# Gate and up products of a feed-forward block: a weight sum by an accumulating transfer, six wide products in 17 blocks, and two pairs of products with their wide matmuls in one row

## The chip, the cores and the metric

The kernel runs as one program on one NeuronCore of a Trainium2 chip. Its engines are TensorE (PE, its weight loads PEld), VectorE (DVE), ScalarE (ACT), GpSimd (POOL) and SyncE (SP); each takes its own instructions in order, and semaphores join them. The metric is the device time of one execution in microseconds, the median of several runs.

## The reference

One decoder layer on a 512 x 1024 stream in float32. The change lies in its third sublayer, the SwiGLU feed-forward with a hidden width of 2816:

```python
hf = rms_norm(x, norm_ffn[l])
gate, up = jnp.split(hf @ w_ffn_in[l], 2, axis=-1)
x = x + (jax.nn.silu(gate) * up) @ w_ffn_out[l]
return rms_norm(x, norm_final)
```

The parts before it (a mixer of stick-breaking attention and a short convolution, then a cross-attention into 256 memory tokens) are the same in both kernels.

## The kernel before

Every float32 product is made from a high and a low part in a rounded 32-bit format: high x high, high x low, low x high. ScalarE casts the high part, VectorE subtracts it from the source to get the low part (`rest_of`, line 1005). The gate and up weights are worked in 22 blocks of 128 hidden columns (`NF`), one block m after another. A block's product is a 2 x 2 matrix of submatrices over two halves of the contraction and of the tokens, and it is computed with seven half-size products (Winograd's form of Strassen's method), numbered 0 to 6. The token side of the seven (`x2f`, made by `forms_of`, line 699) is ready before the stage.

Weight side of block m. `ffn_load` (line 847) loads `wg` (two submatrices) and `ws` (one submatrix twice) on SP's queue and accumulates two more into `ws` with a transfer on POOL's queue. `load_corner` (line 865) loads the submatrix a22. Three VectorE or transfer sums make the rest: `sum_third` (line 872) overwrites the first half of `wg` with the weight of product 3, and `sum_last` (line 876) adds the two halves of `wg` into the second half of the corner tile. Casts: `pair_cast(m, 0)` makes the weights of products 0 and 1 from `wg`, `pair_cast(m, 1)` those of 4 and 2 from `ws`, `pair_cast(m, 2)` those of 5 and 6 from the corner tile, `third_cast` that of 3. There are six input buffers for `wg` and `ws`, three blocks' worth.

A product (line 902) has four steps k over the contraction. A narrow product issues three matmuls of 256 columns in each: 12. Where the token side stands as high and low part beside each other, it is wide: one matmul of 512 columns with the weight's high part, and later one of 256 with its low part: 4 and 4. A wide product leaves two halves in the bank that must be added when it is read. Products 1, 2 and 6 are wide in all blocks, 5 in the blocks of `WIDE` (5 to 18), the others narrow.

Banks: products 0, 3, 4 and 5 accumulate in one PSUM bank z, product 1 has v, products 2 and 6 accumulate in y. After each of 0, 3, 4 ScalarE copies what z holds (`reads`, line 939; with 5 wide, its upper half too), since the running sums are needed; VectorE adds those copies to y and v (`joined_halves`, line 935, two 256-wide additions). `evict` (line 956) scales the gate by the norm's factor (part 0), takes silu on ScalarE (part 1) and multiplies with up (part 2).

The order is written by hand: `uses` (line 980) is the order of products, for a block m

```python
[(m, 3), (m, 2), (m, 4), (m + 1, 0), (m + 1, 1), (m, 5), (m, 6)]
```

and `todo` holds, by place in `uses`, what ScalarE and VectorE do behind that product; `made(n, cast, ...)` puts a cast at place n and its low part one place later. TensorE, ScalarE and VectorE keep this order exactly. In what follows "a block" of the order is one such row of seven products.

Of the kernel before, what the change touches and what calls it, by code (L numbers as in the profile page):

```python
# [44 lines left out]
def hybrid_layer(ctx: ExitStack, tc: tile.TileContext, xT_d, memT_d, mem_d, cols_d, wv_d, win_d,  # L45
# [653 lines left out]
    def forms_of(xe, xo):  # L699

        b11, b12, b21, b22 = xe[:, :HS], xe[:, HS:], xo[:, :HS], xo[:, HS:]
        c, d = f(unit("c1")), f(unit("c2"))
        n1, t3, n2, t4 = c[:, :HS], c[:, HS:], d[:, :HS], d[:, HS:]
        nc.vector.tensor_tensor(out=n1, in0=b11, in1=b12, op=ALU.subtract)
        nc.vector.tensor_tensor(out=t3, in0=b22, in1=b12, op=ALU.subtract)
        nc.vector.scalar_tensor_tensor(out=n2, in0=n1, scalar=-1.0, in1=b22, op0=ALU.mult,  # L708
                                       op1=ALU.subtract)
        nc.vector.scalar_tensor_tensor(out=t4, in0=n2, scalar=-1.0, in1=b21, op0=ALU.mult,  # L710
                                       op1=ALU.subtract)
        u = unit("xf")
# [12 lines left out]
        third, fifth = beside(n2, "xd"), beside(t4, "xd")  # L725
        last = beside(b22, "xo")
        return [(u[:, a], u[:, b]), first, second, third[:2], fourth[:2], fifth, last]

    def residual(w_dram, act, old, gain, pairs=False):

# [112 lines left out]

    KP = KD // 2
    raws, corners = {}, {}

    def ffn_load(m):

# [26 lines left out]

    def sum_last(m, eng=nc.vector):
        wg = raws[m][0]
        eng.tensor_tensor(out=corners[m][:, 1, :], in0=wg[:, 0, :], in1=wg[:, 1, :], op=ALU.add)

    wforms = {}  # L880

    def pair_cast(m, which):

        raw = (*raws[m], corners[m])[which]
        hi = wpool.tile([P, 2, 512], F32R, tag="wh", name=nm("wf"))
        lo = wpool.tile([P, 2, 512], F32R, tag="wl", name=nm("wf"))
        nc.scalar.copy(hi, raw)
# [14 lines left out]
    def product(ps, m, i, ks=range(KP)):  # L902

        rests = []
        for k in ks:
            hi, lo = (w[:, k * P:(k + 1) * P] for w in wforms[m, i])
            xh, xl, *both = x2f[k][i]
            if both and (i != 5 or m in WIDE):
                nc.tensor.matmul(ps, hi, both[0], start=i < 3 and k == 0, stop=False,  # L909
                                 skip_group_check=True)  # L910
                rests.append((ps[:, :HS], lo, xh))
                continue
            for j, (a, b) in enumerate(((hi, xh), (hi, xl), (lo, xh))):
                nc.tensor.matmul(ps[:, :HS], a, b, start=i < 3 and k == 0 and j == 0,  # L914
                                 stop=k == KP - 1 and j == 2, skip_group_check=True)
        for operands in rests:
            nc.tensor.matmul(*operands, start=False,  # L917
                             stop=ks[-1] == KP - 1 and operands is rests[-1],
                             skip_group_check=True)

    WIDE = range(5, NF - 3)
    banks, silus = {}, []
    acts = {}

# [14 lines left out]
    def reads(m, i):  # L939

        b = banks[m]
        z, s, t = b["z"][:, :HS], b["s"], b["t"]
        if i == 5 and m in WIDE:
            nc.scalar.copy(s[:, :HS], b["z"][:, HS:])
        elif i in (0, 3, 4):
            nc.scalar.copy((s[:, :HS], None, None, s[:, HS:], t[:, :HS])[i], z)  # L946
        elif i == 1:
            joined_halves(b["g"][:, :HS], b["v"], s[:, :HS])
        elif i == 6:
            joined_halves(b["g"][:, HS:], b["y"], s[:, HS:])  # L950

    def second(m):
        b = banks[m]
        joined_halves(b["t"][:, HS:], b["y"], b["t"][:, :HS])

    def evict(m, part):
# [6 lines left out]
        else:  # L963
# [3 lines left out]
            to = slice(odd * HS, (odd + 1) * HS)  # L967
            first = b["z"][:, :HS]
            if m in WIDE:
                first = b["s"][:, :HS]  # L970
# [8 lines left out]

    uses = [(0, 0), (0, 1), (0, 2), (1, 0), (1, 1), (0, 3), (1, 3), (0, 4), (1, 2), (0, 5), (0, 6),  # L980
            (1, 4), (2, 0), (2, 1), (1, 5), (1, 6)]
    for m in range(2, NF - 1):
# [158 lines left out]
    for m in range(1, NF - 1):  # L1141
        p = {i: uses.index((m, i)) for i in range(2, 7)}
        q = {i: uses.index((m + 1, i)) for i in range(2)}
        if m > 1:
            at(p[3], lambda m=m: sum_third(m + 1))
            at(p[3], lambda m=m: evict(m - 1, 0))
            at(p[2], lambda m=m: evict(m - 1, 1))
            at(q[0], lambda m=m: evict(m - 1, 2))
            made(p[3], pair_cast, m, 2)
            made(p[2], third_cast, m + 1)  # L1150
        else:
            made(p[4], third_cast, m + 1)
        at(p[4], lambda m=m: second(m))
        if m + 2 < NF:
            at(p[4], lambda m=m: load_corner(m + 2))
        made(q[0], pair_cast, m + 1, 1, late=2)
        at(q[1] if m < NF - 2 else p[4], lambda m=m: sum_last(m + 1))
# [36 lines left out]
    with tc.manual_schedule(engines={mybir.EngineType.PE, mybir.EngineType.Activation,  # L1194
# [6 lines left out]
        for n, (m, i) in enumerate(uses):  # L1201
            if n == 3:
                product(banks[m]["z"], m, i, range(KP - 1, KP))
            elif n > 3:
                product(bank_of(m, i), m, i)
            reads(m, i)
            for part in todo.get(n, ()):
                part()
            if n == 6:
                mean2 = mean2()  # L1210
            elif n == 8:
                mean2 = mean2[0]("r0b", bank=mmtile, later=True)
            elif n == 9:
                r2b[0] = mean2()
                turn_r2()
# [319 lines left out]
```

## Time and profile before

| | |
|---|---|
| median of 3 runs | 839.92 us (839.05 to 839.99) |
| profiled execution | 838.75 us, its span 837.0 us |
| mean granted TensorE clock | 0.998 |
| gate and up stage | from 502 to 721 us of the span, 22 blocks |
| busy in the span: PE, DVE, ACT, POOL | 828.8, 684.6, 463.9, 161.2 us |

A row of the timeline gives start and length of equal instructions that follow each other, then engine, line, operation, out<-in and shape, and in brackets the engine's idle time before it and what ended it. Names are without buffer numbers: z, y, v are banks, sa, sb and fg VectorE's and ScalarE's working tiles, wf a weight form, wg, ws and a the weight tiles (a: the corner tile), xf, xo, xc, xd the token forms. A group row gives the count, the busy time and, after the comma, the mean length of one in ns. The length of a matmul is longer than its distance to the next, since matmuls overlap; starts are compared instead. A block is the time from one product 3 to the next.

### The profile page before, as it was taken

What the parts mean: (1) busy time and instruction counts of PE and PEld (TensorE: products, weight loads), DVE (VectorE), ACT (ScalarE), POOL (GpSimd) and SP (SyncE); (2) the same over time, 40 slices, a digit from 0 to 9 for tenths busy, and PEclk for the clock granted to TensorE, in tenths of its full rate; (3) what the DMA queues carried; (4) which work ended last, traced back from release to release, by engine and by line L of the source; (5) the groups of instructions that cost most, each with busy time, mean ns of one, the idle gap of its engine ahead of it and who ended that gap; (6) DMA issues with size and microseconds to landing.
All of it is one profiled execution on the core that took longest, in us unless ns stands there. A gap on an engine that the chain in (4) does not pass through costs nothing.

```text
span 837.0 us, 11962 instructions
## 1 busy us (share of the span) xinstructions
PE 828.8 (99%) x4374; PEld 714.1 (85%) x4374; DVE 684.6 (82%) x1086; ACT 463.9 (55%) x796; POOL 161.2 (19%) x168
## 2 busy tenths in 40 slices
PE   9999999999999999999999999999999999999996
PEld 7888888888888888888888789999999999888885
DVE  7879899996756576587555698999999999999886
ACT  7567868674332355434444566645555555576654
POOL 0011131110566630173000031111111110000401
PEclk9999999999999999999999999999999999999999
DMA  8552435235687865566431326677767673465552
GB/s 303 155 166 101 122 111 103 74 115 174 228 312 276 304 249 188 182 233 249 148 82 51 101 51 161 167 184 200 197 180 197 176 184 95 170 213 197 180 183 101
DMA packets 51357, 143.69 MB, mean 172 GB/s; under 512 B 5761, under 2 KB 7041, under 8 KB 48482
## 3 DMA queue, kind: packets, MB, share of 16 engines
q1 hardware_dynamic: 41650, 107.89, 38.2%
q0 software_dynamic: 9360, 34.75, 15.8%
q8 instruction: 34, 0.56, 0.3%
q10 hardware_dynamic: 288, 0.28, 0.1%
q14 instruction: 25, 0.20, 0.1%
HBM read 125.20 MB, written 13.64 MB: 166 GB/s over the span
## 4 chain that ended last, share of the span: by engine, by line
PE 99%; DVE 0%; ACT 0%; DVEq 0%; issue 0%
PE z L914 13%; PE p L1228 12%; PE pr L161 8%; PE pr L162 8%; PE pr L163 8%; PE y L909 5%; PE r L162 3%; PE r L163 3%; PE r L161 3%; PE v L288 3%; PE y L917 2%; PE v L909 2%; PE km L666 2%; PE mq L163 2%; PE mq L161 2%; PE mq L162 2%
## 5 line engine op out<-in xcount | busy, mean ns | idle before, releaser
L156 ACT CAST wh<-wr 128x1024 fp32r<-128x1024 f32 x84 | 88.0, 1051 | 144.2 <-issue 80.0
L157 DVE TENSOR_TENSOR wl<-wr,wh 128x1024 fp32r<-128x1024 f32 x84 | 111.0, 1321 | 32.0 <-ACT wh L156 31.9
L161 PE MATMUL pr<-xgh,wh 128*128 128x512 f32 x288 | 112.8, 392 | 0.0
L162 PE MATMUL pr<-xgl,wh 128*128 128x512 f32 x288 | 112.4, 390 | 0.0
L163 PE MATMUL pr<-xgh,wl 128*128 128x512 f32 x288 | 112.3, 390 | 0.0
L611 POOL TENSOR_TENSOR pre<-pre 128x512 f32<-128x512 f32 x44 | 70.9, 1616 | 31.5 <-DMA pre<-in_w_ffn_out_dram 29.2
L862 POOL DMA_DIRECT2D ws<-in_w_ffn_in_dram x22 | 26.6, 1209 | 248.5 <-DVE c L708 54.0
L163 PEld LDWEIGHTS pr<-xgh,wl 128*128 128x128 f32 x288 | 54.1, 188 | 11.5
L161 PEld LDWEIGHTS pr<-xgh,wh 128*128 128x128 f32 x288 | 54.1, 188 | 10.6
L162 PEld LDWEIGHTS pr<-xgl,wh 128*128 128x128 f32 x288 | 54.1, 188 | 10.5
L914 PE MATMUL z<-xd,wf 128*128 128x256 f32 x360 | 47.5, 282 | 0.0
L946 ACT COPY sa<-z 128x256 f32<-128x256 f32 x44 | 16.4, 373 | 51.9 <-PE z L914 51.9
L914 PEld LDWEIGHTS z<-xd,wf 128*128 128x128 f32 x360 | 45.0, 190 | 0.1
L1006 DVE TENSOR_TENSOR wf<-wg,wf 128x1024 fp32r<-128x1024 f32 (+1 forms) x44 | 43.1, 978 | 1.5
L1006 DVE TENSOR_TENSOR wl<-wr,wh 128x1024 fp32r<-128x1024 f32 x33 | 41.0, 1242 | 1.8 <-ACT wh L1073 1.8
L1073 ACT CAST wh<-wr 128x1024 fp32r<-128x1024 f32 x33 | 34.5, 1050 | 5.3 <-ACT f01h L1002 2.6
L914 PE MATMUL z<-xf,wf 128*128 128x256 f32 x264 | 35.4, 283 | 0.0
L914 PE MATMUL z<-xc,wf 128*128 128x256 f32 x264 | 35.1, 283 | 0.0
L914 PEld LDWEIGHTS z<-xf,wf 128*128 128x128 f32 x264 | 33.4, 192 | 0.1
L914 PEld LDWEIGHTS z<-xc,wf 128*128 128x128 f32 x264 | 33.0, 190 | 0.0
L368 DVE TENSOR_TENSOR g<-pr,r0b 128x512 f32<-128x512 f32 x16 | 11.0, 687 | 23.5 <-PE pr L163 23.5
L417 POOL TENSOR_SCALAR_AFFINE_SELECT e<-e 128x128 f32<-128x128 f32 (+1 forms) x24 | 10.7, 447 | 86.6 <-DVE e L470 86.6
(356 smaller groups left out, 2239.9 us busy)
## 6 DMA issues: line engine op xcount, KB each, us to landing
wr<-in_w_in_dram SPq DMA_DIRECT2D x36, 512.0 KB, 3.4
pre<-in_w_ffn_out_dram POOLq DMA_DIRECT2D x11, 1024.0 KB, 8.0
sums<-pre POOLq DMA_DIRECT2D x11, 1024.0 KB, 5.0
ws<-in_w_ffn_in_dram SPq DMA_DIRECT2D x22, 512.0 KB, 4.8
wg<-in_w_ffn_in_dram SPq DMA_DIRECT2D x22, 512.0 KB, 4.7
ws<-in_w_ffn_in_dram POOLq DMA_DIRECT2D x22, 512.0 KB, 5.7
wr<-sums SPq DMA_DIRECT2D x22, 512.0 KB, 4.0
wr<-in_w_ffn_out_dram SPq DMA_DIRECT2D x16, 512.0 KB, 3.7
```

Source lines behind the costliest of these rows:

```text
L156: after(nc.scalar.copy(h2, raw), lead[-1:])
L157: lows.append(nc.vector.tensor_tensor(out=l2, in0=raw, in1=f(h2), op=ALU.subtract))
L161: nc.tensor.matmul(ps, a[0], b[0], start=start, stop=False, **kw)
L162: nc.tensor.matmul(ps, a[0], b[1], start=False, stop=False, **kw)
L163: nc.tensor.matmul(ps, a[1], b[0], start=False, stop=stop, **kw)
L611: nc.gpsimd.tensor_tensor(out=t[:, a, :], in0=t[:, a, :], in1=t[:, b, :], op=ALU.add)
L862: nc.gpsimd.dma_start(s13, a[:, 0:4:3, :], accum_op=ALU.add)
L909: nc.tensor.matmul(ps, hi, both[0], start=i < 3 and k == 0, stop=False, skip_group_check=True)
L914: nc.tensor.matmul(ps[:, :HS], a, b, start=i < 3 and k == 0 and j == 0, stop=k == KP - 1 and j == 2, skip_group_check=True)
L1006: nc.vector.tensor_tensor(out=lo, in0=src, in1=f(hi), op=ALU.subtract)
L1073: nc.scalar.copy(hi, raw)
L1228: nc.tensor.matmul(res[i][s2], a[:, ts], b, start=j == 0 and n == 0, stop=n == 2 and j == (BEHIND - 1 if (i, s2) == (5, 1) else NJ - 1))
```

## The change

Five things change, all in this stage.

1. In blocks 3 to 20 (`OWN`) `sum_last` is no VectorE addition but a transfer on POOL's queue, which accumulates the first half of `wg` onto its second half in place. `load_corner` then loads a22 over the first half of `wg` (SP's queue), so that `wg` itself becomes the source of `pair_cast(m, 2)`. The sum is issued behind `sum_third`, the corner load behind product 5 of the block before.
2. Products 3 and 4 are wide as well in the blocks of `WIDE`, which now are 3 to 19. There products 1 to 6 are wide, six of seven.
3. In these blocks ScalarE's copies behind 3 and 4 are 512 wide, and the two pairs of 256-wide additions on y become `folded`: one 512-wide addition of the bank and the copy, then one 256-wide addition of the two halves.
4. In these blocks the order is 3, 2, next block's 0, 4, next block's 1, 5, 6. Products 3 and 2, and 5 and 6, are issued together: eight 512-wide matmuls, then four 256-wide ones of the first and four of the second.
5. In `OWN` the cast of `pair_cast(m, 2)` moves from behind product 3 to behind product 4.

```diff
+    OWN = range(3, NF - 1)
...
     def load_corner(m):
+        if m in OWN:
+            nc.sync.dma_start(raws[m][0][:, 0, :], wfi_d[m][:, 3 * 512:])
+            return
...
     def sum_last(m, eng=nc.vector):
         wg = raws[m][0]
+        if m in OWN:
+            nc.gpsimd.dma_start(wg[:, 1, :], wg[:, 0, :], accum_op=ALU.add)
+            return
...
-        raw = (*raws[m], corners[m])[which]
+        raw = (*raws[m], raws[m][0] if m in OWN else corners[m])[which]
...
-            if both and (i != 5 or m in WIDE):
+            if both and (i not in (3, 4, 5) or m in WIDE):
...
-        for operands in rests:
-            nc.tensor.matmul(*operands, start=False,
-                             stop=ks[-1] == KP - 1 and operands is rests[-1],
-                             skip_group_check=True)
+        def ends():
+            for operands in rests:
+                nc.tensor.matmul(*operands, start=False,
+                                 stop=ks[-1] == KP - 1 and operands is rests[-1],
+                                 skip_group_check=True)
+        if later:
+            return ends
+        ends()
-    WIDE = range(5, NF - 3)
+    WIDE = range(3, NF - 2)
...
-        if i == 5 and m in WIDE:
-            nc.scalar.copy(s[:, :HS], b["z"][:, HS:])
+        if m in WIDE and i in (3, 4):
+            nc.scalar.copy((s, t)[i - 3], b["z"])
+        elif m in WIDE and i == 5:
+            nc.scalar.copy(t[:, :HS], b["z"][:, HS:])
+        elif m in WIDE and i == 6:
+            folded(b["g"][:, HS:], b["y"], s)
...
+    def folded(out_, bank, old):
+        nc.vector.tensor_tensor(out=old, in0=bank, in1=old, op=ALU.add)
+        nc.vector.tensor_tensor(out=out_, in0=old[:, :HS], in1=old[:, HS:], op=ALU.add)
...
     for m in range(2, NF - 1):
-        uses += [(m, 3), (m, 2), (m, 4), (m + 1, 0), (m + 1, 1), (m, 5), (m, 6)]
+        order = [(m, 3), (m, 2), (m, 4), (m + 1, 0), (m + 1, 1), (m, 5), (m, 6)]
+        if m in WIDE:
+            order[2:4] = order[3:1:-1]
+            beside_next |= {(m, 3), (m, 5)}
+        uses += order
...
             at(p[3], lambda m=m: sum_third(m + 1))
+            if m + 1 in OWN:
+                at(p[3], lambda m=m: sum_last(m + 1))
+                at(p[5], lambda m=m: load_corner(m + 1))
...
-            made(p[3], pair_cast, m, 2)
+            made(p[4] if m in OWN else p[3], pair_cast, m, 2)
...
+            elif uses[n - 1] in beside_next:
+                ends[1]()
+            elif (m, i) in beside_next:
+                ends = [product(bank_of(*use), *use, later=True) for use in uses[n:n + 2]]
+                ends[0]()
```

The instruction order of ScalarE over one block in the middle of the stage, before. z1211 is the bank of this block, z1229 that of the next; a221194 is this block's corner tile (its cast is that of `pair_cast(m, 2)`), wg1203 and ws1202 belong to the next block, wg1221 to the one after.

```order
L946 COPY sa1212_6153<-z1211_6152 128x256
L887 CAST wf1224_6234<-a221194_6037 128x1024
L962 ACTIVATE fg1201_6062<-fg1201_6062 128x512
L895 CAST wf1227_6248<-wg1203_6075 128x512
L946 COPY sb1213_6154<-z1211_6152 128x256
L946 COPY sa1230_6269<-z1229_6268 128x256
L887 CAST wf1232_6287<-ws1202_6073 128x1024
L944 COPY sa1212_6153<-z1211_6152 128x256
L887 CAST wf1238_6318<-wg1221_6191 128x1024
```

The same of the changed kernel. z1198 is the bank of this block, z1215 of the next; wg1178 is this block's `wg`, now the source of `pair_cast(m, 2)`; wg1193 and ws1192 belong to the next block, wg1210 to the one after.

```order
L957 COPY sa1199_6049<-z1198_6048 128x512
L986 ACTIVATE fg1191_5982<-fg1191_5982 128x512
L902 CAST wf1214_6153<-wg1193_5995 128x512
L963 COPY sa1216_6156<-z1215_6155 128x256
L894 CAST wf1218_6175<-ws1192_5993 128x1024
L957 COPY sb1200_6050<-z1198_6048 128x512
L894 CAST wf1220_6187<-wg1178_5891 128x1024
L959 COPY sb1200_6050<-z1198_6048 128x256
L894 CAST wf1226_6225<-wg1210_6102 128x1024
```

The cast of `pair_cast(m, 2)` stood second, behind the copy of product 3; now it stands behind the copy of product 4, and this copy behind that of the next block's product 0 and the cast of its `ws`.

VectorE from the low part of `pair_cast(m, 2)` to the additions of product 6, before (y1226 is the block's y, v1234 the next block's v, wf1225 the low part of the pair from a221194, wf1233 that from `ws` of the next block):

```order
L1006 TENSOR_TENSOR wf1225_6235<-a221194_6037,wf1224_6234 128x1024
L1006 TENSOR_TENSOR wf1227_6248<-wg1203_6075,wf1227_6248 128x512
L936 TENSOR_TENSOR sb1213_6154<-y1226_6237,sb1213_6154 128x256
L937 TENSOR_TENSOR sb1213_6154<-y1226_6237,sb1213_6154 128x256
L971 TENSOR_TENSOR sa1196_6040<-z1195_6039,sa1196_6040 128x256
L974 SCALAR_TENSOR_TENSOR a11214_6168<-sa1196_6040,fg1201_6062 128x256
L974 SCALAR_TENSOR_TENSOR a21215_6169<-sb1197_6041,fg1201_6062 128x256
L936 TENSOR_TENSOR fg1235_6291<-v1234_6290,sa1230_6269 128x256
L937 TENSOR_TENSOR fg1235_6291<-v1234_6290,fg1235_6291 128x256
L878 TENSOR_TENSOR a221210_6150<-wg1203_6075 128x512
L1006 TENSOR_TENSOR wf1233_6288<-ws1202_6073,wf1232_6287 128x1024
L936 TENSOR_TENSOR fg1219_6178<-y1226_6237,sa1212_6153 128x256
```

And of the changed kernel, from the additions of product 2 to the scaling that ScalarE's silu waits for (y1213 is the block's y, v1222 the next block's v, wf1221 the low part of the pair from wg1178, wf1219 that from `ws` of the next block, wf1227 that of the `wg` after):

```order
L970 TENSOR_TENSOR sb1200_6050<-y1213_6135,sb1200_6050 128x512
L971 TENSOR_TENSOR sb1200_6050<-sb1200_6050 128x256
L949 TENSOR_TENSOR fg1223_6193<-v1222_6192,sa1216_6156 128x256
L950 TENSOR_TENSOR fg1223_6193<-v1222_6192,fg1223_6193 128x256
L1035 TENSOR_TENSOR wf1221_6188<-wg1178_5891,wf1220_6187 128x1024
L1035 TENSOR_TENSOR wf1219_6176<-ws1192_5993,wf1218_6175 128x1024
L970 TENSOR_TENSOR sa1199_6049<-y1213_6135,sa1199_6049 128x512
L971 TENSOR_TENSOR fg1208_6089<-sa1199_6049 128x256
L1035 TENSOR_TENSOR wf1227_6226<-wg1210_6102,wf1226_6225 128x1024
L878 TENSOR_TENSOR wg1210_6102<-ws1209_6100,wg1210_6102 128x512
L984 TENSOR_TENSOR fg1208_6089<-fg1208_6089,r0b1034_4940 128x512
```

Before, the low part of this pair came first, ahead of the halves of product 2, the multiplications of the block before and the additions of v; now it comes behind the fold of product 2 and the additions of v. The addition L878 into the corner tile is gone, and the fold takes the place of the two halves.

More of the change, by code (lines that the diff above doesn't have):

```diff
@@ L726, in forms_of @@
         last = beside(b22, "xo")
-        return [(u[:, a], u[:, b]), first, second, third[:2], fourth[:2], fifth, last]
+        return [(u[:, a], u[:, b]), first, second, third, fourth, fifth, last]
     def residual(w_dram, act, old, gain, pairs=False):
@@ L900, in third_cast, with product @@
         return one_form(m, 3, *((fpool, "wg") if m == NF - 1 else (wpool, ("wh", "wl")[m % 2])))
-    def product(ps, m, i, ks=range(KP)):
+    def product(ps, m, i, ks=range(KP), later=False):
         rests = []
@@ L969, in evict @@
             if m in WIDE:
-                first = b["s"][:, :HS]
+                first = b["t"][:, :HS]
                 nc.vector.tensor_tensor(out=first, in0=b["z"][:, :HS], in1=first, op=ALU.add)
@@ L981, in hybrid_layer @@
             (1, 4), (2, 0), (2, 1), (1, 5), (1, 6)]
+    beside_next = set()
     for m in range(2, NF - 1):
-        uses += [(m, 3), (m, 2), (m, 4), (m + 1, 0), (m + 1, 1), (m, 5), (m, 6)]
+        order = [(m, 3), (m, 2), (m, 4), (m + 1, 0), (m + 1, 1), (m, 5), (m, 6)]
+        if m in WIDE:
+            order[2:4] = order[3:1:-1]
+            beside_next |= {(m, 3), (m, 5)}
+        uses += order
     m = NF - 1
@@ L1153, in hybrid_layer @@
         at(p[4], lambda m=m: second(m))
-        if m + 2 < NF:
+        if m + 2 < NF and m + 2 not in OWN:
             at(p[4], lambda m=m: load_corner(m + 2))
         made(q[0], pair_cast, m + 1, 1, late=2)
-        at(q[1] if m < NF - 2 else p[4], lambda m=m: sum_last(m + 1))
+        if m + 1 not in OWN:
+            at(q[1] if m < NF - 2 else p[4], lambda m=m: sum_last(m + 1))
         if m + 2 < NF:
```

2 lines of the change are left out of this document (added).

## Prediction

> **What bounds the kernel now.** I read the shares first, then the clock and the chain, then one block of the gate and up stage in order of time.
>
> ```profile
> PE 828.8 (99%) x4374; PEld 714.1 (85%) x4374; DVE 684.6 (82%) x1086; ACT 463.9 (55%) x796; POOL 161.2 (19%) x168
> PEclk9999999999999999999999999999999999999999
> PE 99%; DVE 0%; ACT 0%; DVEq 0%; issue 0%
> ```
>
> TensorE is never without work and the chain that ended last is TensorE alone. So the change gains only what it takes from TensorE, and loses whatever makes TensorE wait. The windows view gives the stage (502 to 721 us) and one block of it; its columns are length, PE, PEld, DVE, ACT, POOL, clock, DMA share, GB/s:
>
> ```profile
> 502.00:721.00 219.00, 219.00 (x1532) 204.79 (x1531) 210.53 (x365) 121.49 (x205) 25.33 (x23) 1.00 0.65 174
> 595.05:604.96 9.91, 9.91 (x70) 9.21 (x69) 9.55 (x18) 5.44 (x10) 1.20 (x1) 1.00 0.77 205
> ```
>
> VectorE works 9.55 of 9.91 us: there is no wait on PE, but almost no slack behind it. The same block in order of time, TensorE (start, length):
>
> ```profile
> 595.05 1.60 PE L914 MATMUL z<-xd,wf 128*128 128x256 f32 x12
> 596.48 1.09 PE L909 MATMUL y<-xc,wf 128*128 128x512 f32 x4
> 597.41 0.63 PE L917 MATMUL y<-xc,wf 128*128 128x256 f32 x4
> 597.88 1.59 PE L914 MATMUL z<-xc,wf 128*128 128x256 f32 x12
> 599.31 1.60 PE L914 MATMUL z<-xf,wf 128*128 128x256 f32 x12
> 600.75 1.09 PE L909 MATMUL v<-xo,wf 128*128 128x512 f32 x4
> 601.68 0.63 PE L917 MATMUL v<-xo,wf 128*128 128x256 f32 x4
> 602.15 1.09 PE L909 MATMUL z<-xd,wf 128*128 128x512 f32 x4
> 603.56 1.09 PE L909 MATMUL y<-xo,wf 128*128 128x512 f32 x4
> 604.96 1.59 PE L914 MATMUL z<-xd,wf 128*128 128x256 f32 x12
> ```
>
> From start to start a narrow product takes 1.43 us (595.05 to 596.48), a wide one 1.40 (596.48 to 597.88). Its four last, narrow matmuls take 0.47.
>
> **TensorE's gain.** 37 products turn wide: 3 and 4 in 17 blocks, 5 in three more (blocks 3, 4 and 19). At 0.03 us each that is 1.1 us. The new row order of wide matmuls saves nothing more: a wide matmul behind a narrow one starts at the same distance as behind a wide one (1.40 us for y, v and z alike). So 1.1 us is all that can be won, 0.13% of 839.92; about 0.2% is what a measurement of this kernel can tell from no change.
>
> **VectorE's balance.** Per block it loses one sum and gets two wide additions for four narrow ones:
>
> ```profile
> L1006 DVE TENSOR_TENSOR wf<-ws,wf 128x1024 fp32r<-128x1024 f32 x20 | 24.4, 1218 | 0.0
> L874 DVE TENSOR_TENSOR wg<-ws,wg 128x512 f32<-128x512 f32 x20 | 13.8, 692 | 0.6
> L960 DVE TENSOR_TENSOR fg<-fg,r0b 128x512 f32<-128x512 f32 x20 | 13.7, 685 | 0.0
> L878 DVE TENSOR_TENSOR a<-wg 128x512 f32<-128x512 f32 x20 | 13.6, 681 | 0.0
> L937 DVE TENSOR_TENSOR sb<-y,sb 128x256 f32<-128x256 f32 x21 | 8.9, 424 | 0.7
> L368 DVE TENSOR_TENSOR g<-pr,r0b 128x512 f32<-128x512 f32 x16 | 11.0, 687 | 23.5 <-PE pr L163 23.5
> 597.90 0.68 DVE L960 TENSOR_TENSOR fg<-fg,r0b 128x512 f32<-128x512 f32 x1
> 598.51 1.22 DVE L1006 TENSOR_TENSOR wf<-a,wf 128x1024 fp32r<-128x1024 f32 x1
> 600.41 0.42 DVE L936 TENSOR_TENSOR sb<-y,sb 128x256 f32<-128x256 f32 x1
> 600.86 0.42 DVE L937 TENSOR_TENSOR sb<-y,sb 128x256 f32<-128x256 f32 x1
> ```
>
> An instruction starts 0.08 us before the end of an independent one (598.51 against 597.90+0.68), and 0.03 after the end of one it depends on. A pair of halves costs 0.42+0.03+0.42; a fold (`folded`, one 512-wide addition, taken as 0.69 by L368, which also reads PSUM, then a 256-wide one) costs 0.69+0.03+0.42. Two folds add 0.54, the sum takes off 0.60. In total VectorE is as full as before; what matters is where its work stands.
>
> **Where the order goes wrong.** ScalarE in the same block:
>
> ```profile
> 596.68 0.37 ACT L946 COPY sa<-z 128x256 f32<-128x256 f32 x1 [1.46 <-PE z L914]
> 596.95 1.06 ACT L887 CAST wf<-a 128x1024 fp32r<-128x1024 f32 x1
> 598.62 0.64 ACT L962 ACTIVATE fg<-fg 128x512 f32<-128x512 f32 x1 [0.62 <-DVE fg L960]
> 599.16 0.60 ACT L895 CAST wf<-wg 128x512 fp32r<-128x512 f32 x1
> 599.67 0.37 ACT L946 COPY sb<-z 128x256 f32<-128x256 f32 x1
> 601.01 0.37 ACT L946 COPY sa<-z 128x256 f32<-128x256 f32 x1 [0.97 <-PE z L914]
> 601.27 1.05 ACT L887 CAST wf<-ws 128x1024 fp32r<-128x1024 f32 x1
> ```
>
> The second row is the cast for products 5 and 6. It ends at 598.01; product 5 starts at 602.15, 4.1 us later. The change puts this cast behind the copy of product 4, and the copy of product 4 behind product 0 of the next block. Between product 4 and product 5 TensorE now has one product, 1.40 us. In that time ScalarE must do: start 0.20 us after TensorE has gone on (596.48 to 596.68), copy 512 columns from PSUM, cast 1.06, and let TensorE restart. The nearest rows for the wide copy and the restart:
>
> ```profile
> L1273 ACT COPY s<-p 128x512 f32<-128x512 f32 x2 | 1.1, 584 | 0.0
> 460.16 0.59 ACT L179 CAST pth<-pt 128x512 fp32r<-128x512 f32 x1 [1.41 <-PE pt L829]
> 460.80 0.50 PE L161 MATMUL om<-pth,vmh 128*128 128x512 f32 x1
> L914 PEld LDWEIGHTS z<-xd,wf 128*128 128x128 f32 x360 | 45.0, 190 | 0.1
> ```
>
> The copy is 0.58, less 0.10 overlap with what follows it (599.16 against 598.62+0.64). The restart is 0.05 here, where the cast made the moving operand; a stationary one must also be loaded, up to 0.19 more. I take 0.13. Sum: 0.20+0.48+1.06+0.13 = 1.87 against 1.40: 0.47 us of idle TensorE in each of 17 blocks. Nothing covers it.
>
> **It closes a loop.** Behind that late cast VectorE makes the low parts, and behind those stands what feeds the next copy. One turn, following who waits for whom:
> - VectorE ends the scaling `evict(m-1, 0)`; ScalarE starts silu 0.04 later.
> - ScalarE: silu 0.64, third cast 0.60, copy of product 0 0.37, cast of `ws` 1.05, copy of product 4 0.58, less four overlaps of 0.10: 2.84.
> - VectorE: 0.04, fold of product 2 1.14, the two additions of product 1 0.87-0.08, low part of pair 2 1.22-0.08: 3.11.
> - TensorE, waiting for that low part: restart 0.13, the eight narrow matmuls of 5 and 6 0.94, read 0.20 later: 1.27 (VectorE's low part of the `ws` pair, 1.14, fits beside it).
> - VectorE: fold of product 6 1.14, low part of pair 0 1.22-0.08, `sum_third` 0.03+0.69, the scaling 0.69-0.08: 3.61.
>
> Sum 0.04+2.84+3.11+1.27+3.61 = 10.87 us for a block, where TensorE needs 6×1.40+1.43 = 9.83 and took 9.91. So 0.96 more in each of 17 blocks: 16.3 us, with the gain of the wide products already in it. Before, the cast stood two products earlier, so no such loop was closed.
>
> **The hand-over.** Block 20 keeps the old order of products but has the moved cast. From the end of its scaling to the low part that product 5 needs: silu and third cast 0.04+1.14; then on VectorE the third's low part 0.04+0.69, the halves of product 2 0.79, `sum_last(21)` 0.60, the three instructions of `evict(19, 2)` 0.33+0.45+0.34, the low part 1.14, restart 0.13: 5.7 us. The scaling ends 0.20+3.61 = 3.8 after the block begins, so the low part is there at 9.5; TensorE comes to it after 3 narrow and 2 wide products and two matmuls, 4.29+2.80+0.24 = 7.3. That is 2.2 us, once.
>
> **The sum transfer** itself I cost at nothing:
>
> ```profile
> L862 POOL DMA_DIRECT2D ws<-in_w_ffn_in_dram x17 | 20.5, 1208 | 141.4 <-DVE wf L1006 45.1 <-DVE sb L936 36.5 <-DMA ws<-in_w_ffn_in_dram 21.3
> ws<-in_w_ffn_in_dram POOLq DMA_DIRECT2D x17, 512.0 KB, 5.7
> a<-in_w_ffn_in_dram SPq DMA_DIRECT2D x19, 256.0 KB, 2.6
> ```
>
> It moves 256 KB with an addition: between 2.6 us (plain, same size) and 5.7 (accumulating, twice the size). I allow 5.7, then 2.6 for the corner's load that waits for it on SP's queue. It starts at the end of `sum_third`, 3.2 after a block begins; the cast that needs both starts 6.6 into the next block, 14.3 later. So 6 us are spare. Behind the corner's load on SP's queue stand the next `wg` and `ws` loads, which are first read a block later and more. On POOL's queue the accumulation into `ws` stands behind it, one issue (1.2) later; its `sum_third` comes a block later, 10.9, against 1.2+5.7 and the load in front of it. If that cover is gone, see the third rival. The same row shows POOL at 1.21 us per issue while VectorE is 96% busy. The Trainium skill (SBUF — State Buffer, "SBUF: two separate sides") speaks against such a transfer: GpSimd cannot write its descriptors while VectorE holds the shared port in a two-port operation. By that rule the sums would come late, and the time would be that of the third rival; the row shows no such hold.
>
> **Sum.** 838.75 (the profiled execution; its span is 837.0) + 16.3 + 2.2 = 857.25. That run lies 1.2 under the median of 839.92, so on the median: **858.4 us**. With a restart of 0.05 to 0.24 in the loop and the hand-over between 0 and 2.2 the bounds are 855 to 860.
>
> **Rivals.**
> 1. *Only the direct wait counts.* VectorE catches up, the loop doesn't close, each block loses 0.47: 8.0, less 1.1: 846.8. For it: VectorE's sum of work is no larger. Against it: its 9.55 of 9.91. Chance 0.08.
> 2. *No wait: the other side.* The cast comes in time and only the 1.1 stays: 838.8. This decides where copy and cast end within 1.40-0.13 = 1.27 us of product 4 and a turn takes under 9.83; my rows give 1.74 and 10.87. It would need ScalarE's in-order copy to be far shorter than L1273. Chance 0.04.
> 3. *The transfers are late.* If sum and corner take over 6 us more than allowed, or `ws` comes after its `sum_third`, VectorE waits too. `ws` issues on POOL already waited for loads (21.3 us in four or so blocks). Lateness of 1 to 6 us would be paid where the new scheme starts, less in later blocks, which are longer: 859.5 to 865. Chance 0.10.
> 4. *The clock falls.* With TensorE idle twice a block the granted clock could drop; at half speed 17 blocks of 9.83 take 167 us more, about 1025 us. The clock row holds 9 even in the last slice, where TensorE is busy 6 tenths. Chance 0.02. The Trainium skill (TensorE: Matmul & The Clock Gate, "A second HAM failure mode: psum-queue depth-cycling") describes frequent micro-idles that make the clock oscillate; no row here shows it.
>
> The forecast itself has 0.76. The range takes its bounds, most of the third rival, and on the low side a loop that closes only in part: 853 to 865. Under 838.2 nothing leads but an error in all of this: faster 0.01; same 0.03 (the second rival); slower 0.96.
>
> **What would show it.** Right: blocks of about 10.9 us in 17 of 22, two idle places of TensorE in each, the first before product 5 and ended by ScalarE's cast, the second, smaller, before its narrow matmuls and ended by VectorE; ScalarE's cast directly behind the copy of product 4. A wide product still 1.40. Wrong: blocks under 10 us, idle places ended by a DMA, or a clock under 9.

## The result, and the profile after

859.13 us, median of 4 runs (858.49 to 860.02), against 839.60 for the kernel before on the same chip: ratio 1.0234, 95% interval 1.0217 to 1.0250. The forecast was 858.4 (853 to 865). The profiled execution took 860.02, its span is 858.3, 21.3 more than before. From the page of the kernel after:

```profile
PE 838.8 (98%) x4226; PEld 707.6 (82%) x4226; DVE 686.3 (80%) x1071; ACT 470.6 (55%) x799; POOL 172.8 (20%) x186
PE 76%; DVE 15%; ACT 5%; issue 3%; DVEq 0%
```

The chain that ended last was TensorE alone before; now a quarter of it is other engines. VectorE's total has hardly moved (684.6 to 686.3): it isn't more work that costs, but where it stands. TensorE's waits in the whole span:

```profile
PE z L916 <- ACT wf L894: 8.5, 17, 0.5
PE z L921 <- DVE wf L1035: 1.9, 1, 1.9
```

Seventeen waits of 0.5 us for ScalarE's cast, one in each wide block, and one of 1.9 us in the hand-over. A block of the changed order on TensorE (start, length):

```profile
597.18 0.64 PE L926 MATMUL v<-xo,wf 128*128 128x256 f32 x4
598.32 1.20 PE L916 MATMUL z<-xd,wf 128*128 128x512 f32 x4 [0.50 <-ACT wf L894]
599.35 1.08 PE L916 MATMUL y<-xo,wf 128*128 128x512 f32 x4
600.48 0.74 PE L926 MATMUL z<-xd,wf 128*128 128x256 f32 x4
601.06 0.64 PE L926 MATMUL y<-xo,wf 128*128 128x256 f32 x4
601.54 1.09 PE L916 MATMUL z<-xd,wf 128*128 128x512 f32 x4
...
604.33 1.60 PE L921 MATMUL z<-xf,wf 128*128 128x256 f32 x12
605.77 1.09 PE L916 MATMUL z<-xc,wf 128*128 128x512 f32 x4
...
607.17 1.09 PE L916 MATMUL v<-xo,wf 128*128 128x512 f32 x4
608.10 0.64 PE L926 MATMUL v<-xo,wf 128*128 128x256 f32 x4
```

Undisturbed, four narrow matmuls take 0.47 from start to start (601.06 to 601.54) and four wide ones 0.93 (607.17 to 608.10). Here the first group takes 1.14 (597.18 to 598.32), so 0.67 is lost ahead of product 5; product 5's wide matmuls take 1.03, the next group 1.13 (599.35 to 600.48, a wait of 0.20 ahead of the narrow matmuls), and those 0.58. Together 0.67+0.10+0.20+0.11 = 1.08, and 9.83+1.08 = 10.91: that is the block, 10.91 or 10.92 in all 17 (10.92 here, 597.18 to 608.10). The second idle place, 0.20, is not in the list of waits; it is read from these starts. Taking a block's start at its product 1, the first and the last of the 22 are 17.0 us further apart than before; from the last one to the end of the span it is 3.8 us more (131.0 against 127.2), and 0.5 lies ahead of the stage. 17.0+3.8+0.5 = 21.3.

The chain of waits goes through other engines once per block. One turn of it, late in the stage (start, length, what; the short pieces left out are the rest of each engine's work):

```profile
714.56 0.61 ACT fg L986
...
716.82 0.60 ACT sb L957
...
717.44 0.70 DVE sb L970
...
719.30 1.23 DVE wf L1035
...
720.57 0.74 PE z L926 x4
721.31 0.49 PE y L926 x4
...
721.82 0.70 DVE sa L970
...
722.89 1.23 DVE wf L1035
...
724.14 0.69 DVE wg L878
724.84 0.62 DVE fg L984
...
725.47 0.63 ACT fg L986
```

From silu to silu it is 10.91 us: ScalarE 2.88 (to 717.44), VectorE's fold, v additions and low part 3.13 (to 720.57), the narrow matmuls 1.25 (to 721.82), VectorE's fold, low part, third sum and scaling 3.65.

The hand-over, by windows (length, PE, PEld, DVE, ACT, POOL, clock, DMA share, GB/s):

```profile
729.00:731.00 2.00, 0.13 (x2) 0.00 (x0) 1.97 (x5) 1.94 (x3) 0.00 (x0) 1.00 0.53 162
732.40:735.40 3.00, 3.00 (x15) 2.98 (x14) 2.79 (x3) 0.11 (x1) 0.00 (x0) 0.50 0.41 126
```

TensorE stands still for 2.1 us, and 1.4 us after it starts again its granted clock is 0.50 for 3.0 us: 15 matmuls of 256 columns start there, where at 0.12 each (1.43 us for 12) some 25 would. That is another 1.5 us, for which the prediction has no term. Only this execution has a trace; whether the clock fell in the other three as well is open.

### The profile page after: what moved, and what is told of

It is laid out like the page before. It is cut to its first block, busy times and chain, and to the rows that moved or that the text cites. A ratio compares the mean times of both kernels' runs of the same rounds, so it can differ in the third digit from the quotient of the medians.

```text
span 858.3 us, 11666 instructions
## 1 busy us (share of the span) xinstructions
PE 838.8 (98%) x4226; PEld 707.6 (82%) x4226; DVE 686.3 (80%) x1071; ACT 470.6 (55%) x799; POOL 172.8 (20%) x186
## 4 chain that ended last, share of the span: by engine, by line
PE 76%; DVE 15%; ACT 5%; issue 3%; DVEq 0%
PE p L1266 12%; PE pr L161 8%; PE pr L162 8%; PE pr L163 8%; DVE wf L1035 6%; PE r L162 3%; PE r L163 3%; PE r L161 3%; PE v L288 3%; PE km L666 2%; PE mq L163 2%; PE mq L161 2%; PE mq L162 2%; PE br L162 2%; PE br L161 2%
## 5 line engine op out<-in xcount | busy, mean ns | idle before, releaser
L1035 DVE TENSOR_TENSOR wf<-wg,wf 128x1024 fp32r<-128x1024 f32 (+1 forms) x62 | 64.9, 1046 | 1.4 <-ACT wf L902 1.2
L163 PEld LDWEIGHTS pr<-xgh,wl 128*128 128x128 f32 x288 | 54.1, 188 | 11.5
L863 POOL DMA_DIRECT2D ws<-in_w_ffn_in_dram x22 | 26.7, 1213 | 154.7 <-DVE c L707 53.8
L916 PE MATMUL z<-xd,wf 128*128 128x512 f32 x136 | 38.9, 407 | 8.5 <-ACT wf L894 8.5
L894 ACT CAST wf<-wg 128x1024 fp32r<-128x1024 f32 x40 | 42.1, 1054 | 1.8 <-PE r L162 1.8
L883 POOL DMA_DIRECT2D wg<-wg x18 | 16.6, 925 | 102.8 <-DVE wg L878 73.6
L916 PEld LDWEIGHTS z<-xd,wf 128*128 128x128 f32 x136 | 23.1, 188 | 14.9 <-ACT wf L894 11.9
L959 ACT COPY sb<-z 128x256 f32<-128x256 f32 x17 | 6.3, 373 | 50.9 <-PE z L926 50.9
```

The lines of the kernel that those rows point to most:

```text
L163: nc.tensor.matmul(ps, a[1], b[0], start=False, stop=stop, **kw)
L1035: nc.vector.tensor_tensor(out=lo, in0=src, in1=f(hi), op=ALU.subtract)
```

## The experiments

Two theories at first. **Loop**: the late cast closes the loop above, and its turn is the block. **Direct**: only the wait for the cast counts. Later a second question came up: what the transfer costs. The kernel before took 839.55, 839.41 and 839.21 (7 runs each) beside the three groups of runs.

**The cast back in its old place, all else changed.**

```diff
-            made(p[4] if m in OWN else p[3], pair_cast, m, 2)
+            made(p[3], pair_cast, m, 2)
```

> The changed kernel with one thing undone: the cast of the pair for products 5 and 6 stands behind product 3 again in all blocks; the accumulating transfer, the wide products and the new order of products stay. Loop theory (the place of this cast closes a loop through ScalarE, VectorE and TensorE): blocks of 9.83 to 10.0 us in place of 10.92, 839 to 843 us, no idle place before product 5. Transfer theory (the sum by POOL's queue and the corner's load come late): the cast now needs them one and a half products earlier, so it gets worse, 860 us or more, and ScalarE's cast is ended by a DMA. Width theory (512-wide copies and folds overload ScalarE and VectorE): still 855 to 860.

855.6 us (853.1 to 858.73), ratio 1.0188 [1.0159, 1.0218]: a miss for the loop theory's range, and inside that of the width theory, which a later run (wide products alone, 846.40 us) answers. The blocks became irregular, 9.85 to 11.5 and a first one of 15.6. The waits of the trace name the transfer:

```profile
PE z L916 <- ACT sb L957: 6.6, 8, 2.8
ACT wf L894 <- DMA wg<-in_w_ffn_in_dram: 9.0, 11, 3.0
```

The cast now waits for the corner's load, which itself waits for the sum. The transfer does not fit ahead of the cast's old place. So this run doesn't test the loop; it shows what the cast's late place is good for.

**The cast back in block 20 alone** (`p[4] if m in WIDE else p[3]`).

> The changed kernel with the cast behind product 3 again in block 20 alone (where the old order of products holds). If the idle 2.1 us at the hand-over comes from the moved cast, and the half granted clock behind it (0.50 from 732.4 to 735.4 us, about 1.4 us lost) comes from that idle time, both go: 855.3 to 856.2 us, and no stretch at half clock. If only the wait goes and the clock has another cause: 857. If VectorE comes late there for other reasons: 858.5 to 859.5.

856.36 (855.87 to 856.75), ratio 1.0193 [1.0176, 1.0211], 0.2 above the range that was expected if both go. Blocks are 10.91 as before, the stretch behind the last block falls from 131.0 to 127.3, and the clock stays:

```profile
727.40:735.00 7.60, 7.60 (x58) 7.23 (x57) 7.50 (x14) 4.96 (x8) 0.00 (x0) 1.00 0.40 132
```

The hand-over was this cast, and the half clock was its consequence: 3.7 us in the trace, 2.8 between the medians.

**VectorE's sum back, the cast still late** (`OWN = range(0)`, cast at `p[4]` for 3 to 20).

> The changed kernel without the accumulating transfer: the sum is VectorE's addition into a corner tile again in all blocks; the cast stays behind product 4 in blocks 3 to 20, order and widths stay. Loop theory: the addition, 0.60 us, stands in VectorE's leg of the turn, so blocks of 10.9 to 11.5 us, 859 to 869 us. Transfer theory: the cause is gone, 839 to 845 us.

866.32 (865.24 to 867.4; 2 runs), ratio 1.0314; blocks 11.25, 17 waits for the cast of 14.2 us in sum. Without any transfer the loss stays. VectorE's 0.60 makes the block only 0.33 longer, and the traces show why: from the end of the late low part to the fold of product 6 it is 1.31 us in the changed kernel (600.43 to 601.74), where VectorE waits for TensorE's narrow matmuls, and 1.65 here (603.41 to 605.06), where it makes the sum meanwhile.

**The kernel before with nothing but the late cast.**

```diff
-            made(p[3], pair_cast, m, 2)
+            made(p[4] if 3 <= m < NF - 1 else p[3], pair_cast, m, 2)
```

> The kernel before with one thing done: the cast of the pair for products 5 and 6 moved behind product 4 in blocks 3 to 20; no transfer, no new widths, the old order of products. Loop theory in its strong form (VectorE's legs decide, and two products of cover are not enough): blocks near 10.9 us, 855 to 862 us, the wait ended by VectorE's low part. Direct theory (only the time from product 4 to product 5 counts; two products, 2.83 us, cover copy and cast of 1.9): 839 to 842 us. Width and transfer theories: 839 to 841 us.

861.33 (860.81 to 861.84; 2 runs), ratio 1.0255, most blocks of 10.7 and 11.2 in turn. One line moved costs as much as the whole change, and what ends TensorE's waits is the loop's VectorE part, not the cast:

```profile
PE z L917 <- DVE wf L1006: 10.4, 14, 1.0
PE z L914 <- DVE wf L1006: 5.1, 4, 1.9
```

That refutes the direct theory: with no transfer, no wide copies and no new order the block still grows by about one us.

**The transfer alone, on the kernel before, cast in its old place.**

```diff
+    OWN = range(3, NF - 1)
...
+            if m + 1 in OWN:
+                at(p[3], lambda m=m: sum_last(m + 1))
+                at(p[5], lambda m=m: load_corner(m + 1))
...
```

> The kernel before with the accumulating transfer and the corner load over wg alone: old widths, old order, the cast behind product 3. From the end of sum_third the changed kernel's trace has 0.5 to the issue, 4.7 to the landing of the sum, 4.1 to that of the corner: 9.3 to 9.4 us; the cast of the next block stands about 8.9 behind it. So ScalarE waits some tenths for the transfer in a block; the products behind have 4 us of cover: 840 to 848 us. If the transfer costs nothing by itself: 839 to 840 us. If it is the main cause of the loss: over 855 us.

881.77 (879.85 to 886.68), ratio 1.0513 [1.0480, 1.0547]: outside both ranges, over the 855 that was to make the transfer the main cause, and twice the loss of the whole change. But the two runs before it lose as much as the change with no transfer at all, so this is a loss of another kind. Blocks of 9.91 and of 13.5 to 17.6 alternate, and ScalarE's cast waits for the corner's load:

```profile
ACT wf L894 <- DMA wg<-in_w_ffn_in_dram: 56.3, 13, 8.0
```

What delays that load came out only with later runs.

**Wide products and new order alone** (`OWN = range(0)`, which puts the cast back as well).

> The changed kernel without the transfer (VectorE's addition into the corner tile in all blocks) and with the cast behind product 3: the six wide products and the new order alone. VectorE has 9.55 and 0.54 more, 10.1 us a block against TensorE's 9.83: by its sum of work 842 to 848 us. If the new widths and order overload it in another way: over 850 us. If they cost nothing: 838.5 to 840 us.

846.40 (845.91 to 846.68), ratio 1.0081 [1.0064, 1.0098]; blocks of 10.11 and 10.52 in turn. Two of them:

```profile
600.00:620.60 20.60, 20.59 (x121) 17.69 (x121) 20.09 (x34) 11.43 (x18) 2.41 (x2) 1.00 0.72 177
```

VectorE works 20.09 of 20.60 us, 10.05 a block, more than the 9.91 that a block took before. With the sum left to it, VectorE's work no longer fits in the old block; that is what the transfer takes off. TensorE shows no wait in this stretch, so that VectorE sets its length is read from the sums of work and was not tried by itself.

**The changed kernel without the paired rows** (`beside_next` left empty: each product issues its own eight matmuls).

> The changed kernel with the two rows of wide matmuls undone: each product's narrow matmuls directly follow its wide ones; all else stays, the cast too. Loop theory: behind VectorE's low part now stand the four narrow matmuls of 5, the four wide and the four narrow of 6, 0.93 us more in TensorE's leg, so a turn of 11.85 in place of 10.92 and about 875 us. If the loop is not what sets the block (transfers or sheer width do): 857 to 861 us.

910.65 (909.25 to 912.04; 2 runs), ratio 1.0848, outside both ranges. The first three blocks were 11.85, 11.84 and 11.84, the loop's turn for this order; then blocks of 11.8 to 17.2 followed, 35 us more than the loop explains. GpSimd's and SyncE's issues there:

```profile
642.51 1.21 POOL L863 DMA_DIRECT2D ws<-in_w_ffn_in_dram  x1 [13.11 <-DMA ws<-in_w_ffn_in_dram]
643.23 1.43 POOL L883 DMA_DIRECT2D wg<-wg  x1
655.94 1.20 POOL L863 DMA_DIRECT2D ws<-in_w_ffn_in_dram  x1 [11.28 <-DMA ws<-in_w_ffn_in_dram]
656.65 1.43 POOL L883 DMA_DIRECT2D wg<-wg  x1
```
```profile
649.55 0.33 SPq L869 DMA_DIRECT2D wg<-in_w_ffn_in_dram  x1
649.98 0.37 SPq L858 DMA_DIRECT2D wg<-in_w_ffn_in_dram  x1
650.45 0.38 SPq L854 DMA_DIRECT2D ws<-in_w_ffn_in_dram  x1
```

Each sum (L883) goes out directly behind an accumulation into `ws` (L863) for which GpSimd had waited. A second loop: sum 643.23, corner load 649.55, the next `ws` load behind it 650.45, its accumulation 655.94, the next sum 656.65: 13.4 us. GpSimd's order is why; here it is against the changed kernel's (minus: the changed kernel, plus: this run):

```
 L883 DMA wg_5030<-wg_5030 128x512
 L863 DMA ws_5256<-in_w_ffn_in_dram 128x2x512
+L863 DMA ws_5360<-in_w_ffn_in_dram 128x2x512
 L883 DMA wg_5150<-wg_5150 128x512
-L863 DMA ws_5360<-in_w_ffn_in_dram 128x2x512
```

The accumulation of the `ws` that stands behind sum k's corner load comes ahead of sum k+1 instead of behind it. In the run with the transfer alone, two accumulations and two sums stood in a row. Nobody wrote these orders: GpSimd's and SyncE's are the scheduler's. So both runs were put right in this one respect, with every other engine's order unchanged.

Not all of the 35 us is waiting. The longer of TensorE's idle places in this run, 2.3 to 4.8 us, have stretches at half the granted clock beside them, as the clock row of its page shows (tenths, 40 slices of 22.7 us):

```profile
PEclk9999999999999999999999999978999899999999
```

Summed over windows of 0.25 us (TensorE's busy time times the missing share of the clock), these stretches cost an estimated 17 us, against 1.7 in the changed kernel. In the run with the transfer alone it is some 14 of its 42 us. They follow from the waits, and so from the queues.

**The same without paired rows, GpSimd's order put back.**

```diff
...
-        nc.gpsimd.dma_start(s13, a[:, 0:4:3, :], accum_op=ALU.add)
+        i = nc.gpsimd.dma_start(s13, a[:, 0:4:3, :], accum_op=ALU.add)
+        if m > 5 and m - 2 in sums_at:
+            after(i, [sums_at[m - 2]])
...
```

`sums_at` keeps the sums' instructions; `after` only sets the order of the two in the queue.

> The changed kernel without the paired rows, as in the run before it that took 910.65 us, with one thing put back: the weight sum's transfer stands ahead of the accumulating load in GpSimd's queue, as it does in the changed kernel; the order on all other engines is that of the 910.65 us run. Theory A (the loop sets the block, and the surplus over 875 us came from a second loop of two in-order queues: sum, corner load, next load behind it on SyncE's queue, accumulating load behind that on GpSimd's, next sum behind that, 13.4 to 15.4 us a turn): blocks of 11.8 to 11.9 us throughout, 872 to 878 us. Rival B (the transfers are too slow by themselves at this block length): irregular blocks stay, ScalarE's cast still waits for the corner's load, above 890 us.

874.95 (873.82 to 876.32), ratio 1.0425 [1.0409, 1.0441]; blocks 11.81 to 11.84 throughout. The 35 us came of the two queues, with the half clock that followed their waits, and what is left is the loop, 17 times 0.92 over the changed kernel.

**The transfer alone, GpSimd's order put back.**

> The kernel before with the transfer alone and the cast in its old place, as in the run that took 881.77 us, but with the weight sums and the accumulating loads in strict turn in GpSimd's queue; all other engines in the order of that run. Theory A (all of its 42 us came from GpSimd's order, where two loads and two sums stood in a row): no long blocks, 840 to 846 us. Theory B (the chain of the sum and the corner's load, some 9.4 us from VectorE's third sum, ends after the cast's old place in any order): ScalarE's cast goes on waiting for the corner's load, 850 to 862 us, like the changed kernel with its cast moved back, 855.6.

845.92 (844.2 to 848.87), ratio 1.0090 [1.0070, 1.0110]. 36 of its 42 us were GpSimd's order; the mean granted clock is 0.998 again, from 0.980. Some 6.7 us stay, in blocks of 9.91 to 10.9, and the cast still waits for the corner's load:

```profile
ACT wf L896 <- DMA wg<-in_w_ffn_in_dram: 36.2, 15, 3.5
PE z L923 <- ACT sb L955: 1.1, 2, 0.7
PE z L918 <- ACT sb L955: 0.9, 4, 0.3
```

Most of that wait is ScalarE's own idle time, and little of it reaches TensorE: 2.0 us of TensorE's waits name ScalarE, and the other 4.7 were not traced to a cause. Theory A's range holds the median, but the cause that it names for all of it accounts for six sevenths; theory B's wait is there, at a smaller price.

**The third sum behind the scaling** (`evict(m - 1, 0)` ahead of `sum_third(m + 1)`, else the changed kernel): takes the sum's 0.72 out of the loop.

> The changed kernel with two VectorE instructions exchanged: the scaling that silu waits for ahead of sum_third. No work is added or taken away. Loop theory: silu now runs beside sum_third, and the turn loses up to 0.5 us: blocks of 10.4 to 10.7 us, 850 to 855 us. Any theory of too much work or of late transfers: no change, 858 to 860 us (the sum transfer even starts 0.6 later).

856.93 (853.99 and 859.87), ratio 1.0208 [1.0167, 1.0250]. The steady blocks are 10.64, 0.28 less; but three blocks are 11.4 to 15.7, since the sum starts later and ScalarE's cast waits four times for the corner's load (5.9 us). The time lies between the two expectations and the two executions are 5.9 us apart, so it is the steady block that answers: the loop gives, by less than the sum's length, and the transfer's slack is used up. The trace of a steady block shows what holds it then. ScalarE's copies of products 0 and 4 start 0.20 behind the end of these products on TensorE (604.34 and 605.74): silu no longer delays them. A shorter ring is left. From the end of product 4 the copy, the fold, the two additions and the low part take 3.95 us to the narrow matmuls of 5 (605.54 to 609.49), where TensorE has 1.40+1.86 = 3.26 of work. 0.69 and the 0.11 of the slower narrow matmuls make 9.83+0.80 = 10.63, against 10.64 measured.

**Two casts of ScalarE exchanged**, so that VectorE makes the transferred pair's low part ahead of the fold that reads the copy of product 4 (the fold of product 2 above) and not behind it. In block 20 the cast goes back behind product 3, as in the run on block 20 alone.

```diff
-            made(p[4] if m in OWN else p[3], pair_cast, m, 2)
+            made(q[0] if m in WIDE else p[3], pair_cast, m, 2)
...
-        made(q[0], pair_cast, m + 1, 1, late=2)
+        made(p[4] if m in WIDE else q[0], pair_cast, m + 1, 1, late=1 if m in WIDE else 2)
```

> The changed kernel with two casts of ScalarE exchanged in the 17 wide blocks: the transferred pair's cast stands ahead of the copy of product 4, the ws pair's behind it, so that VectorE makes the transferred pair's low part ahead of the fold of product 4 and not behind it; in block 20 the cast is behind product 3 as before the change. ScalarE's work in the loop is the same, VectorE's part before the narrow matmuls falls by about 1.9 us. Theory (the loop through the late low part sets the block): loop of some 8.6 to 9 us, no longer binding, blocks of 9.9 to 10.2, 840 to 846 us. Rival 1 (it is the long block of VectorE or ScalarE work, not this loop): blocks of 10.9 stay, 855 to 858 us. Rival 2 (the corner's load is late for a cast some 2.4 us earlier against its landing): single long blocks ended by the corner's load, 846 to 856 us.

849.60 (848.3 to 852.17), ratio 1.0126 [1.0106, 1.0146]. ScalarE does the same work, and most blocks fall from 10.92 to between 10.13 and 10.17, as the theory said; two blocks of 14.3 and 15.0 are the second rival, each with a stretch at half the granted clock, and with them the time misses the theory's 846:

```profile
PE z L916 <- ACT sb L957: 5.2, 3, 2.9
PE y L916 <- DVE sb L970: 0.5, 3, 0.2
ACT wf L894 <- DMA wg<-in_w_ffn_in_dram: 6.2, 3, 3.2
```

Both expectations hold in part. What holds the block at 10.15 was not tried, but the trace shows the place: product 5 no longer waits, and product 6 starts 1.15 instead of 0.93 us behind it (607.42 to 608.57), 0.06 after VectorE's fold of product 2 has read the bank y that product 6 writes. With the 0.10 of a start behind a wait that is 0.32, and 9.83+0.32 = 10.15. This is 9.5 us under the changed kernel, 2.8 of which block 20's cast brought when it was moved alone. No version was found that beats the kernel before: TensorE's gain of 1.1 us is all that there is to win.

## Why the prediction was right

**The loop** (10.87 predicted, 10.91 measured). The four parts of the turn stand in the chain within 0.05 us each: ScalarE 2.84 predicted and 2.88 found, VectorE 3.11 and 3.13, TensorE 1.27 and 1.25, VectorE 3.61 and 3.65 (with the 0.04 between). Within TensorE's part two errors cancel: the restart takes 0.04 and not 0.13, and the eight narrow matmuls 1.05 and not 0.94, since the first four are slow behind their wait. Six runs bear the loop out. The late cast alone makes the longer block on the kernel before; block 20's cast changes nothing in the 17; the block is 0.92 longer without the paired rows (11.84), 0.33 longer with the sum on VectorE and 0.28 shorter with the third sum out of the ring (each less than the instruction's length, for the reasons given there); and the exchange of two casts of equal length opens it.

**The direct wait** (0.47 predicted). It is the larger of the two idle places, ended by ScalarE's cast, as forecast. The profile's wait of 0.50 is not the same measure, since it counts from the end of a matmul; from start to start, as the prediction counts, 0.67 is lost. ScalarE in the block shown:

```profile
606.70 1.05 ACT L894 CAST wf<-ws 128x1024 fp32r<-128x1024 f32 x1
607.65 0.59 ACT L957 COPY sb<-z 128x512 f32<-128x512 f32 x1
608.13 1.06 ACT L894 CAST wf<-wg 128x1024 fp32r<-128x1024 f32 x1
```

TensorE goes on from product 4 at 607.17, and the copy starts 0.48 later, not 0.20: ScalarE is still at the cast of `ws`, which the loop holds up. That is 0.28 more; the restart, 0.05 (609.19 to 609.24), is 0.08 less. So the size of this wait is in part a symptom of the loop, and the late-cast-only kernel has nearly the same block with other waits.

**TensorE's gain.** A wide product still takes 1.40 (605.77 to 607.17). What the step left unsaid is that the wide products do not fit without more: with the sum left to VectorE and the cast in its old place the kernel is 7 us slower than before. No run shows the 1.1 us in its time.

**VectorE's balance** (as full as before): 684.6 and 686.3 us in the span.

**The hand-over** (2.2 predicted). The idle time is 1.92 in the waits, 2.1 in the windows. What was left out is what followed: some 1.5 us at half the granted clock, which no term held. It is most of the 1.6 by which the stretch behind the last block exceeds the forecast's 2.2.

**The transfer at nothing.** True of the changed kernel as it stands. In the block shown the sum goes out at 605.29, the corner's load at 610.11 and lands some 3.8 later, and the cast that needs both starts at 619.05: 5 us spare, where the prediction had 6. From the timeline, one engine each, and from the list of transfers (size, median us to landing):

```profile
605.29 0.90 POOL L883 DMA_DIRECT2D wg<-wg  x1 [4.70 <-DVE wg L878]
```
```profile
610.11 0.33 SPq L869 DMA_DIRECT2D wg<-in_w_ffn_in_dram  x1
```
```profile
619.05 1.06 ACT L894 CAST wf<-wg 128x1024 fp32r<-128x1024 f32 x1
```
```profile
wg<-wg POOLq DMA_DIRECT2D x18, 256.0 KB, 4.7
wg<-in_w_ffn_in_dram SPq DMA_DIRECT2D x18, 256.0 KB, 3.8
```

The sum's median lay in its bounds (4.7 between 2.6 and 5.7, the longest 6.7); the corner's load took 3.8 where 2.6 was allowed. Together that is 8.5 for 8.3. But the prediction took the cast's late place and the transfer as two edits with two prices. They are one: the late place is what buys the transfer its slack. Put back, the cast waits (855.6 us). And the statement that an accumulation on POOL's queue stands one issue behind the sum holds only for the order that the scheduler happened to choose; the other order costs 36 us.

**The port.** The rule of the Trainium skill (SBUF — State Buffer, "SBUF: two separate sides") that would have delayed the sums did not show; it speaks of two-port operations of VectorE, and no run here shows whether these additions are such. The 18 issues of the sum (shortest, median, longest ns), and a block by windows:

```profile
L883 POOL DMA_DIRECT2D wg<-wg x18: 862/897/1398, 532.9 to 714.5; - x18
```
```profile
596.50:607.42 10.92, 10.37 (x62) 8.79 (x61) 9.36 (x16) 5.71 (x10) 2.11 (x2) 1.00 0.88 220
```

An issue takes about 0.9 us while VectorE is busy 9.36 of 10.92 us, and where sums were late (without the paired rows), GpSimd had been waiting for a load.

**The clock** (rival 4). Idle places of 0.2 to 0.7 us twice a block left the granted clock at 1.00 in the stage; the rule of the Trainium skill on micro-idles (TensorE: Matmul & The Clock Gate, "A second HAM failure mode: psum-queue depth-cycling") does not show either, at this size of idle. What the rival left out is a single longer idle place, as in the hand-over.

**The sum.** 16.3+2.2 = 18.5 predicted, 17.0+3.8 in the trace: 0.7 more in the blocks, 1.6 in the hand-over. The other 0.5 of the spans' difference lies ahead of the stage, where the two kernels are the same. On medians it is 19.5, and the forecast was 18.5. That 858.4 comes within 0.7 of the measured 859.13 is partly luck: the terms were 2.3 us short of the trace, but the profiled execution after lies 0.9 above its median and the one before 0.85 under its own, so that the medians show less of it.

## What to carry to other kernels

When an edit moves one instruction of an in-order engine behind another, don't price the wait that it makes: follow the ring of who waits for whom until it comes back to the same place one block later, and add up its turn; where it is longer than the busiest engine's work (here 10.87 against 9.83), that number, not the engines' totals, is the block. A transfer that replaces a cheap addition is bought with slack on its consumer, so look for what was moved to give it that slack. And where sums and loads share in-order queues, check which load stands ahead of which sum: two queues that wait for each other form a ring of their own, and a scheduler may reorder them when something else is edited.

## What the runs showed of the hardware

- A short idle time of TensorE can be followed by a stretch at half the granted clock. In this stage, over all runs, each of the 20 idle places of 2.19 to 5.18 us had such a stretch of 3 us or more beside it. Of eight places between 1.73 and 1.93 us, five had one (1.73 with the late cast alone, 1.79 with the transfer alone, 1.92 in the changed kernel, 1.92 and 1.93 in the two runs without the paired rows) and three had none (1.74 and 1.76 without the paired rows, 1.93 with the late cast alone). The five between 1.17 and 1.35 us had none. Where the idle place was 1.73 to 2.39 us, the clock fell between 0.2 us before the restart and 2.0 us after it. From the late cast alone:

```profile
722.00:725.00 3.00, 3.00 (x12) 2.61 (x11) 1.35 (x3) 0.00 (x0) 0.00 (x0) 0.50 0.33 98
```

  The Trainium skill (TensorE: Matmul & The Clock Gate, "HAM oscillation — how this bites in real kernels") names idle gaps of over some 3.4 us; here half of that sufficed, not every time.
- The first four wide matmuls behind a wait took 1.03 instead of 0.93 us from start to start, the first four narrow ones 0.58 instead of 0.47, beside the wait itself.
- An accumulating transfer of 256 KB between two halves of one tile lands 3.3 to 6.7 us after its issue, median 4.7; an accumulation of 512 KB into `ws` in the changed kernel 6.8.
